# A transformer layer on one core: residual sums kept in the output by accumulating DMAs, and a down projection in 26 sums

## The chip, the core and the metric

The kernel runs on one core of a Trainium2 chip, as one program. The metric is the device time of one execution in microseconds (us). The instructions of each engine (TensorE "PE", VectorE "DVE", ScalarE "ACT", GpSimd "POOL", and SyncE "SP", which here only issues DMAs) run in the order in which they stand in that engine's program. They wait for each other through semaphores.

## What is computed

One layer of a hybrid encoder on 640 tokens (512 of a prompt, 128 of a sample), model width 2048, all in f32. Cut to what matters here:

```
a = rms_norm(x, g_mix);  proj = a @ w_in              # q, k, v, forget, ssm input
merged = concat(rms_norm(attention), rms_norm(s5))    # 2048 wide
h = x + merged @ w_out                                # stage "o"
f = rms_norm(h, g_ffn)
h = h + (silu(f @ w_gate) * (f @ w_up)) @ w_down      # stages "g", "u" and "d"
gate = sigmoid(rms_norm(h, g_ple) @ w_ple_gate)       # stage "p"
return h + gate * (p_i @ w_ple_proj)
```

## The kernel before

**Tiling.** Everything is kept transposed: rows are features, columns are the 640 tokens. From the o stage on, each f32 product is three matmuls, since every operand is cut into a high and a low part: wh by k0, wh by k1, wl by k0 (L1205, L1206, L1207). A block of two by two is multiplied with seven products instead of eight (Strassen in Winograd's form). The outputs of a stage come 256 rows at a time. One such pair of 128 rows, `j`, is one **sum** (`strassen`): seven PSUM tiles are accumulated over a number of weight **units**, each with 42 matmuls of 128x128 by 128x320, and then put together into a pair tile by two copies on ACT (L1232, L1234), six additions on DVE (L1233, L1235 to L1239) and one on POOL (L1240). The names say stage and sum: `o4` is the fifth sum of the o stage, `ro4` its result. All pair tiles (`r...`, `x...`, `hx...`, `hy...`, `pj...`) share two buffers.

**Stages.** o: 8 sums of 4 units. Then 22 times a g sum and a u sum, 4 units each. d: the down projection, 8 output pairs over 11 units each. An output pair's 11 units are cut into several sums (cells), because only 8 of the operand tiles `kt` fit; in the kernel before that is 28 sums in seven steps, each of them four pairs over the same units. p: 8 sums of 4 units.

**Weights.** `Ring` loads each unit (512 KB, SP queue, `wst`, two buffers), forms the Winograd combinations on DVE (`ws`, L109 to L112, four of 128x256), and cuts it: ACT writes `wh` (L86, one of 128x768 and one of 128x1024) and DVE writes `wl` (L87, the same two). `wh` and `wl` have two buffers, so a unit is cut while the two before it are in use. Units are numbered through the whole program: o is 84 to 115, d begins at 292, p is 380 to 411.

**What follows a sum.** In o the input rows `x` are read and added (L1280), the pair is stored to `h_dr`, scaled (ACT, L1267, twice 128x640), combined into the seven Winograd operands (`winograd_rows`, L118 to L121) and stored to `fc_dr`. Its squares go into the RMS sum (ACT L1249, DVE L1253 and L1254). The g stage later fetches these operands (`kf`) and cuts each into its two parts (`whole`: ACT L1050 and DVE L1051, a piece of 128x1280 and one of 128x960). In d all sums but a pair's last are added into `h_dr` by an accumulating DMA on the POOL queue (L1346). After a pair's last sum the rows are read back on the SP queue (`hx`), added (L1350), stored to `h_dr` (the profile gives `h2_dr` that name too), scaled, combined, and stored to `hc_dr` or cut directly (`kh`). In p each result is normalised, gated, multiplied by `pj`, and added on POOL to `hy`, the rows read back from DRAM (L1373). Then it is stored.

**Order.** A scheduler sets the order of each engine's instructions from dependencies and its own planned times; the text of the program gives priorities and no fixed order. A change of the text so moves instructions everywhere.

Of the kernel before, what the change touches and what calls it, by code (L numbers as in the profile page):

```python
# [9 lines left out]
F32 = mybir.dt.float32  # L10
# [4 lines left out]
OP = mybir.AluOpType  # L15
# [113 lines left out]
def down_cells():  # L129

    low, high = range(4), range(4, 8)
    steps = [(low, 0, 2), (high, 0, 4), (low, 2, 6), (high, 4, 8), (low, 6, 8), (high, 8, 11), (low, 8, 11)]
    return [(j, range(a, b), a == 0, b == FT // 4) for js, a, b in steps for j in js]

# [28 lines left out]
def hybrid_step(ctx: ExitStack, tc: tile.TileContext, io):  # L165
# [21 lines left out]
    cells = down_cells()  # L187
    units += [(1, io["w_down"][j, u]) for j, us, _, _ in cells for u in us]
    units += [(1, io["w_pg"][j, u]) for j in range(8) for u in (2, 3, 0, 1)]
    ring = Ring(nc, stp, units)  # L190
# [5 lines left out]
    m_dr = dp.tile([D, NTOK], F32, name="m_dr")  # L196
    h_dr = dp.tile([D, NTOK], F32, name="h_dr")
    h2_dr = dp.tile([D, NTOK], F32, name="h2_dr")
    tc_dr = dp.tile([FT // 2, P, 7, NH2], F32, name="tc_dr")
# [706 lines left out]
    def attention(h):  # L906
# [133 lines left out]
    def scale_group(s, name):  # L1040
# [135 lines left out]

    later = {}

    def fetch(name, slot, dram, i, late=False):
        k = kp_tile("k" + name, slot)  # L1180
        x = k[:, 1].bitcast(F32)
        nc.sync.dma_start(x, dram[i])
        if late:
            later.setdefault(i // 2 - 2, []).append(lambda: whole(k, x))
            return k
        return whole(k, x)

    def cut_late(u):
        for f in later.pop(u, ()):
            with tc.issue_after(ring.done[0]), tc.issue_after(ring.done[1]):  # L1190
                f()

    def products(name, kps, after=None, order=None):
# [74 lines left out]

    fk = []
    for j in range(8):  # L1270
        after = None
        if j == 7:
            def after(u):
                for i in (2 * u, 2 * u + 1):
                    if i < 7:
                        fk.append(fetch(f"f{i}", i, fc_dr, i, late=i == 6))
        r = strassen(f"o{j}", mk, after)
        x = pair(f"x{j}")
        nc.sync.dma_start(x, io["xT"][2 * j : 2 * j + 2].rearrange("a p n -> p a n"))
        nc.vector.tensor_tensor(r, r, x, op=OP.add)  # L1280
        c = seven(f"c{j}")
        scaled(c, r, gffn, j)
        if j < 7:
            keep(nc.vector, c, fc_dr, j)
        else:
            winograd_rows(nc.vector, c[:, :4], c[:, 4:])
            kf7 = kp_tile("kf7", 7)
            fk.append(kf7)
            later.setdefault(1, []).append(lambda: whole(kf7, c))
        nc.sync.dma_start(rows(h_dr, j), r)  # L1290
        squares(ssqh, r, x, j == 0)

# [9 lines left out]
    for f in range(FT // 2):  # L1302
        z = strassen(f"g{f}", fk, cut_late if f == 0 else None)
        if f == 0:
            scale_rows(ssqh, D)
        by_rows(z, ssqh)
        nc.scalar.activation(z, z, AF.Silu)
        after = None
        if f == FT // 2 - 1:
            def after(u):  # L1310
                if u < 2:
                    next_t()
        c = seven(f"t{f}")
# [8 lines left out]
    for j, us, _, _ in cells:  # L1322
        for u in us:
            uses[u] = uses.get(u, 0) + 1
    hk, hslot = {}, {4: 6, 5: 7, 6: 0, 7: 1, 0: 2, 1: 3, 2: 4, 3: 5}
    ready = []

    def next_h():
        i = ready.pop(0)
        hk[i] = fetch(f"h{i}", hslot[i], hc_dr, i)  # L1330

    for n, (j, us, first, last) in enumerate(cells):
        def after(i, us=us, n=n):
            uses[us[i]] -= 1
            if not uses[us[i]] and n < len(cells) - 4:
                next_t()
            if n < 2 and i:
                next_t()
            if n == len(cells) - 1:
                for _ in range(min(2, 3 - i)):  # L1340
                    if ready:
                        next_h()
# [8 lines left out]
        c = seven(f"hc{j}")  # L1351
        scaled(c, r, gple, j)
        if j in (3, 4, 5):
            winograd_rows(nc.vector, c[:, :4], c[:, 4:])
            hk[j] = whole(kp_tile(f"kh{j}", hslot[j]), c)
        else:
            keep(nc.vector, c, hc_dr, j)
            ready.append(j)
        nc.sync.dma_start(rows(h2_dr, j), r)
        squares(ssqp, r, x, j == 4)  # L1360
    hk = [hk[i] for i in (4, 5, 6, 7, 0, 1, 2, 3)]
    for j in range(7):
        z = strassen(f"p{j}", hk)
        if j == 0:
# [14 lines left out]
    nc.sync.dma_start(x, rows(pj_dr, 7))  # L1379
    nc.sync.dma_start(y, rows(h2_dr, 7))  # L1380
    ps = products("p7", hk, order=(1, 2, 6, 5, 3, 7, 4))
# [145 lines left out]
```

## Time and profile before

| | us |
|---|---|
| median of 3 runs | 2956.65 |
| lowest, highest | 2954.58, 2957.56 |
| the profiled execution | 2953.62 |
| its span from first to last instruction | 2951.8 |
| 0 to 801.5: input projection, attention, s5 | 801.5 |
| o, with its start | 801.5 to 1036 |
| g and u | 1036 to 2137 |
| d | 2137 to 2714 |
| p | 2714 to 2951.8 |

A time of the profile is counted from the span's start. TensorE is busy for 96% of the span, and its matmuls follow each other without a gap when nothing is missing; what can be lost or won are the places where it waits. PE's busy time counts a matmul as longer when the granted clock is lower, so a stretch is best read by its number of matmuls.

### The profile page before, as it was taken

What the parts mean: (1) busy time and instruction counts of PE and PEld (TensorE: products, weight loads), DVE (VectorE), ACT (ScalarE), POOL (GpSimd) and SP (SyncE); (2) the same over time, 40 slices, a digit from 0 to 9 for tenths busy, and PEclk for the clock granted to TensorE, in tenths of its full rate; (3) what the DMA queues carried; (4) which work ended last, traced back from release to release, by engine and by line L of the source; (5) the groups of instructions that cost most, each with busy time, mean ns of one, the idle gap of its engine ahead of it and who ended that gap; (6) DMA issues with size and microseconds to landing.
All of it is one profiled execution on the core that took longest, in us unless ns stands there. A gap on an engine that the chain in (4) does not pass through costs nothing. (4 is left out here: it accounts for less than half of the span.)

```text
span 2951.8 us, 47685 instructions
## 1 busy us (share of the span) xinstructions
PE 2827.2 (96%) x19051; PEld 2717.0 (92%) x19051; DVE 2265.6 (77%) x3912; ACT 1240.9 (42%) x1627; POOL 420.7 (14%) x463
## 2 busy tenths in 40 slices
PE   8899999998799989999999999999999999999998
PEld 6789998887789889999999999999989999998898
DVE  8939354455698888787878787878886877899888
ACT  4333365555643453333333333333433444355433
POOL 6612310001000001010101010101020100100111
PEclk9999999999989999999999999999999999999999
DMA  5565744547534633233323333333554445647444
GB/s 168 153 180 159 224 168 173 176 145 260 191 133 172 223 139 123 100 116 101 118 100 118 101 117 102 117 102 117 190 159 139 144 158 175 164 153 271 139 156 143
DMA packets 137487, 449.19 MB, mean 152 GB/s; under 512 B 14096, under 2 KB 34672, under 8 KB 124464
## 3 DMA queue, kind: packets, MB, share of 16 engines
q1 hardware_dynamic: 120032, 396.47, 39.2%
q0 software_dynamic: 15936, 45.47, 6.2%
q10 hardware_dynamic: 1296, 4.20, 0.4%
q8 instruction: 149, 2.44, 0.3%
q14 instruction: 74, 0.61, 0.1%
HBM read 342.25 MB, written 101.18 MB: 150 GB/s over the span
## 5 line engine op out<-in xcount | busy, mean ns | idle before, releaser
L86 ACT ACTIVATE wh<-wst 128x768 fp32r<-128x768 f32 x328 | 276.9, 845 | 659.3 <-issue 319.9
L87 DVE TENSOR_TENSOR wl<-ws,wh 128x1024 fp32r<-128x1024 f32 x328 | 421.0, 1284 | 101.4 <-ACT wh L86 101.0
L86 ACT ACTIVATE wh<-ws 128x1024 fp32r<-128x1024 f32 x328 | 344.6, 1051 | 358.9 <-DVE ws L112 358.9
L87 DVE TENSOR_TENSOR wl<-wst,wh 128x768 fp32r<-128x768 f32 x328 | 337.5, 1029 | 169.3 <-ACT wh L86 169.3
L1205 PE MATMUL d<-kt,wh 128*128 128x320 f32 x1232 | 383.6, 315 | 11.8 <-ACT wh L86 5.1
L1205 PE MATMUL g<-kf,wh 128*128 128x320 f32 x1232 | 381.6, 310 | 5.5 <-ACT wh L86 5.4
L1206 PE MATMUL g<-kf,wh 128*128 128x320 f32 x1232 | 381.1, 310 | 0.0
L1205 PE MATMUL u<-kf,wh 128*128 128x320 f32 x1232 | 380.3, 309 | 0.5 <-DVE rg L1236 0.4
L1206 PE MATMUL d<-kt,wh 128*128 128x320 f32 x1232 | 380.7, 312 | 0.0
L1206 PE MATMUL u<-kf,wh 128*128 128x320 f32 x1232 | 380.1, 309 | 0.0
L1207 PE MATMUL g<-kf,wl 128*128 128x320 f32 x1232 | 375.6, 310 | 4.4 <-DVE wl L87 4.4
L1207 PE MATMUL u<-kf,wl 128*128 128x320 f32 x1232 | 376.1, 309 | 0.6 <-DVE wl L87 0.6
L1207 PE MATMUL d<-kt,wl 128*128 128x320 f32 x1232 | 344.5, 315 | 7.4 <-DVE wl L87 7.3
L1205 PEld LDWEIGHTS d<-kt,wh 128*128 128x128 f32 x1232 | 235.1, 191 | 17.7 <-ACT wh L86 9.7
L1205 PEld LDWEIGHTS g<-kf,wh 128*128 128x128 f32 x1232 | 232.1, 188 | 6.8 <-ACT wh L86 6.8
L1207 PEld LDWEIGHTS g<-kf,wl 128*128 128x128 f32 x1232 | 230.2, 188 | 5.5 <-DVE wl L87 5.2
L1206 PEld LDWEIGHTS d<-kt,wh 128*128 128x128 f32 x1232 | 235.1, 191 | 0.0
L1207 PEld LDWEIGHTS d<-kt,wl 128*128 128x128 f32 x1232 | 224.8, 191 | 11.2 <-DVE wl L87 10.6
L1206 PEld LDWEIGHTS g<-kf,wh 128*128 128x128 f32 x1232 | 232.2, 189 | 0.0
L1205 PEld LDWEIGHTS u<-kf,wh 128*128 128x128 f32 x1232 | 231.2, 188 | 1.0 <-DVE rg L1236 0.7
L1206 PEld LDWEIGHTS u<-kf,wh 128*128 128x128 f32 x1232 | 231.2, 188 | 0.0
L1207 PEld LDWEIGHTS u<-kf,wl 128*128 128x128 f32 x1232 | 230.0, 188 | 0.9 <-DVE wl L87 0.9
(499 smaller groups left out, 5981.2 us busy)
## 6 DMA issues: line engine op xcount, KB each, us to landing
wst<-in_w_gate SPq DMA_DIRECT2D x88, 512.0 KB
wst<-in_w_up SPq DMA_DIRECT2D x88, 512.0 KB
wst<-in_w_down SPq DMA_DIRECT2D x88, 512.0 KB
tc_dr<-t SPq DMA_DIRECT2D x22, 1120.0 KB
kt<-tc_dr SPq DMA_DIRECT2D x22, 1120.0 KB
wst<-in_w_qk SPq DMA_DIRECT2D x32, 512.0 KB
kc<-in_cache_k SPq DMA_DIRECT2D x16, 1024.0 KB
vc<-in_cache_v SPq DMA_DIRECT2D x16, 1024.0 KB
```

Source lines behind the costliest of these rows:

```text
L86: a = nc.scalar.activation(wh[:, part], x, AF.Copy)
L87: b = nc.vector.tensor_tensor(wl[:, part], x, wh[:, part].bitcast(F32), op=OP.subtract)
L1205: nc.tensor.matmul(ps[i], wh[:, a, w], k[:, 0, b], start=f, stop=False)
L1206: nc.tensor.matmul(ps[i], wh[:, a, w], k[:, 1, b], start=False, stop=False)
L1207: nc.tensor.matmul(ps[i], wl[:, a, w], k[:, 0, b], start=False, stop=l)
```

## The change

1. Seven copies, x rows to the output `o_yT`, DRAM to DRAM, 640 KB each, are written into the attention loop on the POOL queue.
2. In o (sums 0 to 6) the addition of `x` and the store to `h_dr` go. The result is added into `o_yT` by an accumulating DMA of the POOL queue, and the sum is read back into a pair tile by a second DMA of that queue (`add_h`). Scaling, combining and squares work on that tile one sum later (`done_o`, after unit 1). The last sum is added on DVE.
3. The cutting of fetched operands is put off: `fetch` only notes it, and `cut_next` does one or two of them after later units.
4. d has 26 sums, in three groups of pairs, (4, 5), (0, 1, 6) and (7, 2, 3). A pair's last sum is also accumulated and read back one sum later; only the very last (pair 5) is added on DVE. Pairs 6 and 7 are cut directly, the others go through `hc_dr`; `kh4` is fetched on the POOL queue.
5. In p the reading of `hy`, the POOL addition and the store become one accumulating DMA.

```diff
-    low, high = range(4), range(4, 8)
-    steps = [(low, 0, 2), (high, 0, 4), (low, 2, 6), (high, 4, 8), (low, 6, 8), (high, 8, 11), (low, 8, 11)]
+    one, two, three = (4, 5), (0, 1, 6), (7, 2, 3)
+    steps = [(one, 0, 2), (two, 0, 3), (three, 0, 4), (one, 2, 6), (two, 3, 7), (three, 4, 8), (one, 6, 8),
+             (two, 7, 11), (three, 8, 11), (one, 8, 11)]
...
-    units += [(1, io["w_pg"][j, u]) for j in range(8) for u in (2, 3, 0, 1)]
+    units += [(1, io["w_pg"][j, u]) for j in range(8) for u in (3, 0, 1, 2)]
...
     for h in range(H):
+        if h:
+            nc.gpsimd.dma_start(io["o_yT"][2 * (h - 1) * P : 2 * h * P, :].rearrange("(a p) n -> a p n", p=P), xrow(h - 1))
...
+    def wait_cut(k, x):
+        uncut[id(k)] = tick[0], lambda: whole(k, x)
+        return k
...
-        return whole(k, x)
+        eng.dma_start(x, dram[i])
+        return wait_cut(k, x)
+
+    def cut_next(n=1, age=2):
+        for key in list(uncut)[:n]:
+            if tick[0] - uncut[key][0] >= age:
+                uncut.pop(key)[1]()
...
+    def add_h(r, j):
+        nc.gpsimd.dma_start(hrow(j), r, accum_op=OP.add)
+        x = pair(f"h{j}")
+        nc.gpsimd.dma_start(x, hrow(j))
+        return x
...
+    def done_o(x, j):
+        c = seven(f"c{j}")
+        scaled(c, x, gffn, j)
+        keep(nc.vector, c, fc_dr, j)
+        squares(ssqh, x, j == 0)
+
     for j in range(8):
...
+            if u == 1 and due:
+                due.pop()()
...
         r = strassen(f"o{j}", mk, after)
-        x = pair(f"x{j}")
-        nc.sync.dma_start(x, io["xT"][2 * j : 2 * j + 2].rearrange("a p n -> p a n"))
-        nc.vector.tensor_tensor(r, r, x, op=OP.add)
-        c = seven(f"c{j}")
-        scaled(c, r, gffn, j)
         if j < 7:
-            keep(nc.vector, c, fc_dr, j)
...
-        nc.sync.dma_start(rows(h_dr, j), r)
-        squares(ssqh, r, x, j == 0)
+            x = add_h(r, j)
+            due.append(lambda x=x, j=j: done_o(x, j))
...
+    def done_h(x, j):
+        c = seven(f"hc{j}")
+        scaled(c, x, gple, j)
+        if j in (6, 7):
+            winograd_rows(nc.vector, c[:, :4], c[:, 4:])
+            hk[j] = wait_cut(kp_tile(f"kh{j}", hslot[j]), c)
+        else:
+            keep(nc.vector, c, hc_dr, j)
+        squares(ssqp, x, j == 0)
...
         if not last:
-            nc.gpsimd.dma_start(rows(h_dr, j), r, accum_op=OP.add)
-            continue
-        x = pair(f"hx{j}")
-        nc.sync.dma_start(x, rows(h_dr, j))
-        nc.vector.tensor_tensor(r, r, x, op=OP.add)
...
-        nc.sync.dma_start(rows(h2_dr, j), r)
-        squares(ssqp, r, x, j == 4)
+            nc.gpsimd.dma_start(hrow(j), r, accum_op=OP.add)
+        elif not end:
+            x = add_h(r, j)
+            due.append(lambda x=x, j=j: done_h(x, j))
...
         nc.vector.tensor_tensor(z, z, x, op=OP.mult)
-        x = pair(f"hy{j}")
-        nc.sync.dma_start(x, rows(h2_dr, j))
-        nc.gpsimd.tensor_tensor(z, z, x, op=OP.add)
-        nc.sync.dma_start(rows(io["o_yT"], j), z)
+        nc.gpsimd.dma_start(hrow(j), z, accum_op=OP.add)
```

**What it does to the order.** First POOL at the program's start: `cb`, `dpad` and `zero` are tables being prepared, `ssq` and `xsq` the RMS sum of the input. Before:

```order
L317 MEMSET zero 128x1024
L408 MEMSET cb 128x2048
L269 TENSOR_TENSOR ssq<-ssq,xsq_169 128x640
L319 DMA dpad<-in_dskip 16x1024
L318 DMA k_dr<-zero 128x1024
L269 TENSOR_TENSOR ssq<-ssq,xsq_397 128x640
```

and now:

```order
L317 MEMSET zero 128x1024
L408 MEMSET cb 128x2048
L1021 DMA o_yT<-in_xT 16x10240 x2
L269 TENSOR_TENSOR ssq<-ssq,xsq_168 128x640
L1021 DMA o_yT<-in_xT 16x10240 x5
L319 DMA dpad<-in_dskip 16x1024
L318 DMA k_dr<-zero 128x1024
L269 TENSOR_TENSOR ssq<-ssq,xsq_396 128x640
```

The copies of the attention loop stand at the start, ahead of the DMAs for `dpad` and `k_dr` and of all but one of the `ssq` additions.

Second, ACT behind the sum o4, whose successor o5 has the units 104 to 107 (a `wh` from `wst` is the 128x768 piece, one from `ws` the 128x1024 piece). Before:

```order
L86 ACTIVATE wh104_9377<-ws104_9379 128x1024
L86 ACTIVATE wh105_9432<-wst105_9333 128x768
L1267 ACTIVATE c4_9459<-ro4_9445,c_g_ffn_134 128x640 x2
L1249 ACTIVATE x4_9456<-ro4_9445 128x1280
L86 ACTIVATE wh106_9520<-wst106_9388 128x768
L86 ACTIVATE wh105_9432<-ws105_9434 128x1024
L86 ACTIVATE wh106_9520<-ws106_9522 128x1024
L86 ACTIVATE wh107_9575<-wst107_9443 128x768
```

and now, from the same place on (L1265 is the squares' instruction, before L1249):

```order
L86 ACTIVATE wh105_9434<-wst105_9335 128x768
L86 ACTIVATE wh105_9434<-ws105_9436 128x1024
L86 ACTIVATE wh106_9510<-wst106_9390 128x768
L86 ACTIVATE wh106_9510<-ws106_9512 128x1024
L1290 ACTIVATE c4_9565<-h4_9459,c_g_ffn_133 128x640 x2
L86 ACTIVATE wh107_9576<-wst107_9445 128x768
L1265 ACTIVATE h4_9459<-h4_9459 128x1280
L86 ACTIVATE wh107_9576<-ws107_9578 128x1024
```

The scaling `c4` stood ahead of the first piece of unit 106; now it stands behind the whole of 106 and ahead of the first piece of 107, the last unit of o5. It reads `h4`, the tile read back, in place of `ro4`.

Third, ACT in the last part of d, behind the sum of pair 6 (`qd` and the rows `rd...<-d...` are the two copies of the sum that follows). Before:

```order
L1267 ACTIVATE hc6_25579<-rd22_25565,c_g_ple_136 128x640 x2
L1249 ACTIVATE hx6_25576<-rd22_25565 128x1280
L86 ACTIVATE wh366_25552<-ws366_25554 128x1024
L1232 ACTIVATE qd23_25764<-d23_1_25591 128x320
L86 ACTIVATE wh368_25695<-wst368_25563 128x768
L86 ACTIVATE wh367_25640<-ws367_25642 128x1024
L86 ACTIVATE wh368_25695<-ws368_25697 128x1024
L1234 ACTIVATE rd23_25763<-d23_3_25593 128x320
L86 ACTIVATE wh369_25750<-wst369_25651 128x768
L86 ACTIVATE wh369_25750<-ws369_25752 128x1024
L86 ACTIVATE wh370_25838<-wst370_25706 128x768
```

and now:

```order
L86 ACTIVATE wh367_25579<-wst367_25459 128x768
L86 ACTIVATE wh367_25579<-ws367_25581 128x1024
L1290 ACTIVATE hc6_25634<-h6_25528,c_g_ple_135 128x640 x2
L86 ACTIVATE wh368_25645<-wst368_25514 128x768
L1265 ACTIVATE h6_25528<-h6_25528 128x1280
L1248 ACTIVATE qd21_25714<-d21_1_25530 128x320
L1059 ACTIVATE kh6_25641<-hc6_25634 128x1280
L1250 ACTIVATE rd21_25713<-d21_3_25532 128x320
L1059 ACTIVATE kh6_25641<-hc6_25634 128x960
L86 ACTIVATE wh368_25645<-ws368_25647 128x1024
L86 ACTIVATE wh369_25700<-wst369_25590 128x768
L86 ACTIVATE wh369_25700<-ws369_25702 128x1024
```

The scaling `hc6` reads the tile read back, and the cutting of `kh6` (L1059), which was done from `hc_dr` much later, now stands right behind it, ahead of the second piece of unit 368.

## Rows read from the trace of the kernel before

**Rows 1.** the page, busy time, share of the span and instructions
```profile
PE 2827.2 (96%) x19051; PEld 2717.0 (92%) x19051; DVE 2265.6 (77%) x3912; ACT 1240.9 (42%) x1627; POOL 420.7 (14%) x463
```

**Rows 2.** stretches: PE, PEld, DVE, ACT, POOL busy (xcount), clock, DMA share, GB/s
```profile
898.70:1003.90 105.20, 99.83 (x673) 98.48 (x673) 88.21 (x149) 43.05 (x52) 3.50 (x4) 1.00 0.47 174
1003.90:1127.20 123.30, 107.94 (x694) 103.78 (x693) 107.24 (x163) 62.96 (x72) 9.61 (x8) 0.97 0.46 171
1127.20:2112.80 985.60, 985.60 (x6722) 985.60 (x6721) 814.42 (x1267) 347.90 (x420) 124.55 (x120) 1.00 0.33 110
2297.90:2578.30 280.40, 271.90 (x1808) 269.58 (x1807) 218.93 (x364) 109.84 (x133) 33.64 (x26) 0.98 0.54 155
2578.30:2713.76 135.46, 130.85 (x859) 125.69 (x858) 125.99 (x211) 66.03 (x80) 7.98 (x7) 1.00 0.54 184
2713.76:2786.20 72.44, 59.91 (x352) 56.61 (x351) 61.67 (x89) 37.98 (x42) 6.85 (x3) 0.91 0.53 197
2786.20:2915.10 128.90, 125.68 (x841) 123.17 (x841) 113.11 (x161) 46.41 (x55) 20.04 (x10) 1.00 0.46 160
```

**Rows 3.** the o stage after one sum's end: start, us, instruction [idle before]
```profile
905.24 0.47 DVE L1239 TENSOR_TENSOR ro<-ro,o 128x320 f32<-128x320 f32 x1
...
907.82 1.55 ACT L1267 ACTIVATE c<-ro,c_g_ffn 128x640 f32<-128x640 f32 x2 [5.28 <-DVE ro L1280]
...
910.44 0.83 ACT L86 ACTIVATE wh<-wst 128x768 fp32r<-128x768 f32 x1
...
911.32 0.42 PE L1205 MATMUL o<-km,wh 128*128 128x320 f32 x1 [1.34 <-ACT wh L86]
...
911.48 0.95 DVE L87 TENSOR_TENSOR wl<-wst,wh 128x768 fp32r<-128x768 f32 x1
```

**Rows 4.** POOL in the down stage, the same columns
```profile
2227.72 1.20 POOL L1346 DMA_DIRECT2D h_dr<-rd  x1 [2.80 <-issue]
...
2250.39 1.20 POOL L1346 DMA_DIRECT2D h_dr<-rd  x1 [0.84 <-POOL rd L1240]
```

**Rows 5.** the tile h_dr: durations of its instructions in ns, issue to landing
```profile
L1346 POOL DMA_DIRECT2D h_dr<-rd x20: 1195/1204/1305, 2168.9 to 2562.9; - x20
...
DMA to landing us min/median/max: 6.6/8.0/14.0
```

**Rows 6.** the DMA issues: KB each, median us to landing
```profile
db<-d_dr POOLq DMA_DIRECT2D x8, 512.0 KB, 5.2
```

**Rows 7.** groups by line in 2172.4:2637, DVE: busy, mean ns
```profile
L1051 DVE TENSOR_TENSOR kt<-kt 128x1280 fp32r<-128x1280 f32 x14 | 20.8, 1489 | 9.5 <-ACT kt L1050 9.5
L1051 DVE TENSOR_TENSOR kt<-kt 128x960 fp32r<-128x960 f32 x14 | 16.1, 1154 | 0.0
```

**Rows 8.** the start of the p stage, the columns of rows 3
```profile
2706.97 0.66 SPq L60 DMA_DIRECT2D wst<-in_w_pg  x1
...
2717.96 0.64 PE L1205 MATMUL p<-kh,wh 128*128 128x320 f32 x1 [3.89 <-ACT wh L86]
```

**Rows 9.** inside the p stage, the same columns
```profile
2799.07 1.22 DVE L87 TENSOR_TENSOR wl<-ws,wh 128x1024 fp32r<-128x1024 f32 x1
...
2799.18 0.38 SPq L1372 DMA_DIRECT2D hy<-h_dr  x1
...
2803.29 3.77 POOL L1373 TENSOR_TENSOR rp<-rp,hy 128x1280 f32<-128x1280 f32 x1 [10.59 <-DMA hy<-h_dr]
...
2804.47 3.40 DVE L87 TENSOR_TENSOR wl<-wst,wh 128x768 fp32r<-128x768 f32 x1 [0.24 <-ACT wh L86]
```

**Rows 10.** groups by line in 2786.2:2915.1: busy, mean ns
```profile
L87 DVE TENSOR_TENSOR wl<-ws,wh 128x1024 fp32r<-128x1024 f32 x20 | 36.3, 1817 | 11.4 <-ACT wh L86 11.3
```

**Rows 11.** table by stretch of the start, the columns of rows 2
```profile
10.00:20.00 10.00, 10.00 (x42) 8.03 (x41) 8.08 (x7) 5.42 (x9) 8.58 (x9) 1.00 1.01 374
20.00:50.00 30.00, 25.18 (x93) 18.96 (x92) 27.84 (x71) 18.63 (x27) 15.48 (x9) 0.89 0.47 156
60.00:90.00 30.00, 20.25 (x98) 16.07 (x97) 29.52 (x69) 4.32 (x7) 20.26 (x24) 0.88 0.37 102
```

More of the change, by code (lines that the diff above doesn't have):

```diff
@@ L1175, in whole, with fetch @@
         return k
-    later = {}
-    def fetch(name, slot, dram, i, late=False):
+    uncut, tick = {}, [0]
+    def wait_cut(k, x):
+        uncut[id(k)] = tick[0], lambda: whole(k, x)
+        return k
+    def fetch(name, slot, dram, i, eng=nc.sync):
         k = kp_tile("k" + name, slot)
         x = k[:, 1].bitcast(F32)
[L1182 to L1185, printed above, removed]
-        return whole(k, x)
[L1188 to L1191, printed above, removed]
+        eng.dma_start(x, dram[i])
[4 more added lines that the diff above has]
+                uncut.pop(key)[1]()
     def products(name, kps, after=None, order=None):
@@ L1310, in after @@
             def after(u):
-                if u < 2:
+                if u < 3:
                     next_t()
+                cut_next((0, 0, 2, 1)[u], 1)
         c = seven(f"t{f}")
@@ L1321, in hybrid_step @@
     uses = {}
-    for j, us, _, _ in cells:
+    for j, us, _ in cells:
         for u in us:
             uses[u] = uses.get(u, 0) + 1
[L1325 to L1333, printed above, removed]
+    hk, hslot = {}, {6: 6, 7: 7, 0: 0, 1: 1, 2: 2, 3: 3, 4: 4, 5: 5}
+    due = []
+    def done_h(x, j):
+        c = seven(f"hc{j}")
+        scaled(c, x, gple, j)
+        if j in (6, 7):
+            winograd_rows(nc.vector, c[:, :4], c[:, 4:])
+            hk[j] = wait_cut(kp_tile(f"kh{j}", hslot[j]), c)
+        else:
+            keep(nc.vector, c, hc_dr, j)
+        squares(ssqp, x, j == 0)
@@ L1334, in after, with next_h @@
+    def next_h(j, eng=nc.sync):
+        hk[j] = fetch(f"h{j}", hslot[j], hc_dr, j, eng)
+    for n, (j, us, last) in enumerate(cells):
+        end = n == len(cells) - 1
+        def after(i, us=us, n=n, end=end):
+            if i == 1 and due:
+                due.pop()()
             uses[us[i]] -= 1
-            if not uses[us[i]] and n < len(cells) - 4:
+            if not uses[us[i]] and us[-1] < FT // 4 - 1:
                 next_t()
-            if n < 2 and i:
+            if n == 0 and not i:
@@ L1338, in after @@
                 next_t()
[L1339 to L1342, printed above, removed]
+            if end:
+                if i == 1:
+                    due.append(pair("h5"))
+                    nc.sync.dma_start(due[0], hrow(5))
+                for k in ((0, 1), (2, 3), (4,))[i]:
+                    next_h(k, nc.gpsimd if k == 4 else nc.sync)
+            cut_next(1, 1 if n < 2 else 2)
         r = strassen(f"d{n}", [tk[i] for u in us for i in (2 * u, 2 * u + 1)], after)
@@ L1359, in hybrid_step @@
-        nc.sync.dma_start(rows(h2_dr, j), r)
-        squares(ssqp, r, x, j == 4)
-    hk = [hk[i] for i in (4, 5, 6, 7, 0, 1, 2, 3)]
+            nc.gpsimd.dma_start(hrow(j), r, accum_op=OP.add)
+        elif not end:
+            x = add_h(r, j)
+            due.append(lambda x=x, j=j: done_h(x, j))
+    x = due.pop()
+    nc.vector.tensor_tensor(x, x, r, op=OP.add)
+    c = seven("hc5")
+    scaled(c, x, gple, 5)
+    nc.gpsimd.dma_start(hrow(5), x)
+    winograd_rows(nc.vector, c[:, :4], c[:, 4:])
@@ L1362, in hybrid_step, with after_p0 @@
+    hk[5] = wait_cut(kp_tile("kh5", hslot[5]), c)
+    hk = [hk[i] for i in (6, 7, 0, 1, 2, 3, 4, 5)]
+    def after_p0(u, x=x):
+        if u == 1:
+            squares(ssqp, x, False)
+        cut_next(1, 0)
     for j in range(7):
-        z = strassen(f"p{j}", hk)
+        z = strassen(f"p{j}", hk, after_p0 if j == 0 else None)
         if j == 0:
@@ L1379, in hybrid_step @@
     nc.sync.dma_start(x, rows(pj_dr, 7))
-    nc.sync.dma_start(y, rows(h2_dr, 7))
+    nc.sync.dma_start(y, hrow(7))
     ps = products("p7", hk, order=(1, 2, 6, 5, 3, 7, 4))
```

67 lines of the change are left out of this document (37 added, 30 removed).

## The prediction

> **What bounds the kernel now.** I read the page first: TensorE is busy for 96% of the span [rows 1]. Then I cut the trace into stretches and counted matmuls in each, because a matmul has a fixed step when nothing is missing. Through the long g and u loop 6722 matmuls take 985.60 us, 0.1466 us each [rows 2], so a unit of 42 takes 6.16 us. What a stretch takes above its count times 0.1466 is its loss, clock drops included. By the other rows of the same table [rows 2]: four sums of o (898.7 to 1003.9) lose 105.2 - 673 x 0.1466 = 6.5 us, 1.6 for each sum; the end of o and the first g and u sums (1003.9 to 1127.2) lose 21.5; g and u nothing; the part of d with the four places where new `kt` are cut (2297.9 to 2578.3) loses 15.3; the last part of d (2578.3 to 2713.8) 9.5; the first sum of p with the end of its transition (2713.8 to 2786.2) 20.8; the other p sums (2786.2 to 2915.1) 5.6. The reader is to see there that DVE is nearly full (107 of 123, 126 of 135 us) in just these stretches, and at 83% in the g and u loop, which loses nothing. So the bound is TensorE, and what it loses it loses where DVE and ACT have, besides each unit's `wh` and `wl`, a burst of other work, or where they stand in line behind something that waits. The removable loss is about 80 us; the change goes at all of these places, and adds waits for DMAs in the same lines.
>
> **Start: seven copies.** They are new. By the order they stand on POOL at about 16 us, right where the DMA engines carry 374 GB/s at a share of 1.01 [rows 11]. 7 x 655,360 bytes = 4.6 MB take 12.3 us at that rate. In the 30 us after that the share is 0.47, so the engines have 16 us free: the copies fit, but the loads of `x` and weights beside them are late. DVE is busy for 27.8 of those 30 us and for 29.5 of the 30 from 60 on [rows 11], so what it loses it doesn't win back soon. Behind the copies on POOL's queue stand the `dpad` and `k_dr` DMAs and the `ssq` additions. Bounds: 0 (all in the free share) and +12 (all on the path). I take **+4.5**, nearer to the free share.
>
> **o, sums 0 to 6: the read-back.** Before, DVE adds `x` and the scaling follows. Now accumulate, read-back, scaling. Let T be the start of the next sum's first unit. In the trace PE waits for 1.34 us until 911.32 at that sum's second unit, so T = 911.32 - 1.34 - 6.16 = 903.8, and the last combination ends at 905.71 = T + 1.9 [rows 3]. The accumulating DMA is issued behind it, without delay or after POOL has sat idle for 2.8 us in place of 0.84 [rows 4]; I take 1.2 us. From issue to landing it takes 6.6 to 14.0, median 8.0, in d [rows 5]. The read-back waits for that; a POOL read of 512 KB takes 5.2 [rows 6], an SP read of 640 KB 4.1 until its reader starts [rows 9], and 5.2 x 640 / 512 = 6.5. I take 5.8. The tile is there at T + 1.9 + 1.2 + 8.0 + 5.8 = T + 16.9. When is it wanted? By the order, ACT's scaling stands ahead of the first `wh` of the next sum's last unit, which begins at T + 3 x 6.16 = T + 18.5. Behind the scaling (1.55) come that `wh` (0.83) and its `wl` (0.95), which PE wants some 0.3 after it starts [rows 3]: the tile is late from T + 18.5 + 0.3 - 1.55 - 0.83 - 0.95 = **T + 15.5** on. So a sum stalls for 1.4 us, and with some 0.4 for work that is ahead in the row when the tile lands (my choice) for 1.8, against 1.6 now: 7 x 0.2, **+1.5**. The DVE addition that goes (7 x 1.48) was work beside a PE that waits for ACT here, so it pays nothing by itself. Bounds: nothing late, -11; the read as slow as the accumulation, 8.0, +17.
>
> What the row shows on the size is 8.0 us for 640 KB with accumulation [rows 5]. The Trainium skill (DMA: Bandwidth & Descriptors, Anatomy of one DMA) fits a POOL DMA by 2.0 us plus bytes / 436e3, which gives 3.5 us as an estimate for each of the two transfers; the tile would come at about T + 10, nothing would stall, and this term would be -11. The trace does not agree for an accumulating one; no run here shows a 640 KB read on POOL.
>
> **End of o, first g.** The squares of the last sum go behind g0's second unit, and the operands are cut one by one. The loss of 21.5 us goes with DVE's excess of work, of which the change takes little (one set of squares, 1.6 us, is put later; the last sum's addition remains): **-2** (-4 to +1).
>
> **d, where `kt` are cut.** A tile costs DVE 1.489 + 1.154 = 2.6 us [rows 7]. Four of them in a row are 10.6 us, beside units of 6.16 us in which DVE has two `wl` (1.22 and 0.95) and four `ws` to make. Four such places make up the loss of 15.3, about 3.8 each. With `cut_next` and the new groups, by the order of DVE, two places stay as they are, at a third the four tiles are apart two by two, and the last two lie inside a sum. I take 1.5 places: **-5.5** (-9 to 0). What is late next there is nothing: steady d sums lose nothing. 26 sums instead of 28 also save two sets of combinations on DVE, beside other work: nothing.
>
> **d, last part.** Before, DVE is full (126.0 of 135.5) and 9.5 us are lost. Away go 7 x 1.48 us of DVE additions, which would pay nearly all of it. In comes the same wait as in o, 7 times, in the row of ACT ahead of a `wh`: 7 x about 1.2 us, less than in o since some sums have three units and others four, so the scaling stands at another place. `hc6` is the worst: the cutting of `kh6` now stands between the two pieces of unit 368, 2.2 us more of ACT. **-1** (-9 to +14).
>
> **p, first sum.** Now PE waits 3.89 us for unit 380, whose load was issued at 2706.97, behind two `kh` loads, and then runs at a lower granted clock, 0.91 over the stretch [rows 2, 8]. The load now stands ahead of the `kh` loads on SP. On the other side `kh0` to `kh5` are all cut here, and `kh4` is fetched on POOL behind the store of `hc4`: **-2** (-7 to +6).
>
> **p, the rest.** POOL's addition (3.77 us) goes. While it runs, DVE's `wl` takes 3.40 us instead of 0.95 [rows 3, 9], and the 20 wide ones take 1.817 on average, where an undisturbed one takes 1.22 [rows 9, 10]: 20 x 0.6 = 12 us of DVE. The loss of 5.6 us goes with it: **-5.2** (-5.6 to 0). The accumulating DMAs end long before the last sum's own stores.
>
> **Sum.** 4.5 + 1.5 - 2 - 5.5 - 1 - 2 - 5.2 = -9.7 us. The profiled execution took 2953.62 (span 2951.8); -9.7 gives 2943.9. The median of the runs, 2956.65, is 3.0 above it: **2947**, 0.3% faster. About 0.2%, 5.9 us, is what a measurement here can tell from no change.
>
> **Rivals.**
>
> *A. The read-back comes late (slower).* The tile is read back 14 times, in o and d, and each time ACT, and behind it the next `wh`, stands in line. Every us later than T + 16.9 costs 14 us; from T + 17.6 on (9.7 / 14 = 0.7 later) the whole gain is gone. For it: landings of up to 14.0 us [rows 5], and the POOL issue that is delayed by 2.8 [rows 4]. Against it: the median of 8.0 is narrow at the lower end, and the SP read of 4.1 [rows 9]. If the read takes 8.0 like the accumulation, 14 x 2.2 = 31 us: 2947 + 31 = **2978**.
>
> *B. The copies starve the start.* All 12 us on the path instead of 4.5: 2947 + 7.5 = **2954.5**, no change. For it: the full DMA engines and DVE [rows 11]. Against it: the free share behind. The Trainium skill (DMA: Bandwidth & Descriptors, Queues, rings and completion order) says that a DMA engine takes queues in turn, packet by packet; the trace of before has no second busy queue there to show it. By that rule the loads beside the copies go at half their pace, which is this rival.
>
> *C. The read-back is early.* Issue at once, 6.6, and 4.1: T + 1.9 + 6.6 + 4.1 = T + 12.6, ahead of T + 15.5. Neither o nor the tail then stalls: 14 x 1.8 = 25 us less, **2922**. The fit of the page above leads here too.
>
> *D. The cutting is not spread.* The change doesn't do at the `kt` places what it says, and the burst stays: 2947 + 5.5 = **2952.5**.
>
> **How the numbers follow.** Forecast 0.40, A 0.24, B 0.14, C 0.17, D 0.05. The forecast's own range is 2936 to 2958 (a few of the bounds above, together), most of it below 2950.7. Faster: 0.28 of the forecast, all of C, a third of B and half of D, 0.52. Slower (above 2962.6): nearly all of A and 0.04 of the rest, 0.27. No change: 0.21. The range reaches from C's value to a read-back 1.6 us late (2947 + 23): 2922 to 2970.
>
> **What would show it.** In the changed kernel: the time from a sum's end to ACT's scaling in o, with PE's wait at the last unit of the next sum; landing times of the accumulating DMAs (8.0) and of the read-back (5.8); the length of 20 to 50 us and the time at which o begins (801.5 now); the loss around each group of new `kt`; no `wl` above 1.3 us in p. A read-back at T + 19 or an o stage that begins 10 us late would make the prediction wrong; so would tail stalls of 3 us at each pair.

## The result and the profile after

The changed kernel takes 3000.9 us (median of 4 runs, 2994.9 to 3007.0), the kernel before in the same session 2955.6: a ratio of 1.0157, 95% interval 1.0144 to 1.0169. By that ratio it is 46 us slower; the median is 54 above the forecast and 31 above the top of the range. The profiled execution is the slowest of the four (3006.96, span 3005.2, 53.4 longer than that of before).

The table by stretch of the changed kernel, with the columns of [rows 2]; the stretches are those of [rows 2], with the start of o as the first row:

```profile
814.30:918.60 104.30, 83.97 (x506) 78.56 (x505) 83.75 (x140) 46.06 (x59) 5.78 (x6) 0.92 0.46 141
918.60:1031.10 112.50, 102.18 (x674) 100.08 (x673) 79.78 (x144) 41.94 (x53) 11.30 (x12) 0.98 0.57 162
1031.10:1158.70 127.60, 110.69 (x663) 105.90 (x662) 102.72 (x153) 61.32 (x68) 15.38 (x11) 0.89 0.48 169
...
2337.40:2593.90 256.50, 250.44 (x1665) 248.24 (x1665) 200.47 (x329) 102.38 (x122) 27.25 (x22) 0.98 0.54 156
2593.90:2767.50 173.60, 153.47 (x968) 148.87 (x967) 123.94 (x219) 67.65 (x82) 22.93 (x20) 0.94 0.52 149
2767.50:2845.20 77.70, 58.27 (x343) 54.91 (x342) 60.80 (x90) 40.86 (x45) 7.81 (x6) 0.85 0.57 194
2845.20:2969.30 124.10, 124.10 (x841) 123.10 (x841) 100.89 (x162) 46.63 (x55) 10.33 (x10) 1.00 0.49 136
```

That first stretch in the kernel before:

```profile
801.50:898.70 97.20, 81.77 (x491) 77.41 (x490) 85.38 (x139) 44.37 (x57) 1.76 (x2) 0.89 0.45 160
```

Length minus count times 0.1466, as in the prediction, gives the losses in us (g and u lose 0.3 at most, before and after):

| stretch | before | after |
|---|---|---|
| time at which o begins | 801.5 | 814.3 |
| o, first three sums | 25.2 | 30.1 |
| o, four sums | 6.5 | 13.7 |
| end of o, first g and u sums | 21.5 | 30.4 |
| d with the new `kt` | 15.3 | 12.4 |
| d, last part | 9.5 | 31.7 |
| first p sum | 20.8 | 27.4 |
| p, the rest | 5.6 | 0.8 |

DVE is less busy than before (123.9 of 173.6 us in the last part of d, where it was 126.0 of 135.5), while more is lost. So the amount of its work is not what costs.

**One sum of o.** Timeline of the changed kernel behind the sum o3 (start, us, instruction, and in brackets the idle time before it):

```profile
950.85 0.47 DVE L1255 TENSOR_TENSOR ro<-ro,o 128x320 f32<-128x320 f32 x1
...
951.88 1.20 POOL L1274 DMA_DIRECT2D o_yT<-ro  x1 [2.43 <-issue]
...
960.31 0.75 POOL L1276 DMA_DIRECT2D h<-o_yT  x1 [7.24 <-issue]
...
965.12 1.55 ACT L1290 ACTIVATE c<-h,c_g_ffn 128x640 f32<-128x640 f32 x2 [7.22 <-DMA h<-o_yT]
...
965.98 0.49 DVE L118 TENSOR_TENSOR c<-c 128x320 f32<-128x320 f32 x1 [6.03 <-ACT c L1290]
...
967.46 0.42 PE L1217 MATMUL o<-km,wh 128*128 128x320 f32 x1 [3.10 <-ACT wh L86]
...
979.56 0.47 DVE L1255 TENSOR_TENSOR ro<-ro,o 128x320 f32<-128x320 f32 x1
...
995.75 0.42 PE L1217 MATMUL o<-km,wh 128*128 128x320 f32 x1 [1.10 <-ACT wh L86]
```

The matmuls of o up to PE's wait at 967.46 (window, length, PE busy and count, clock, DMA share, GB/s):

```profile
814.30:967.45 153.15, 127.76 (x798) 0.94 0.49 145
```

A sum has 168 matmuls, and 798 is 4 x 168 + 126: PE waits 3.10 us just ahead of the last unit of the next sum, which so began at T = 967.46 - 3.10 - 18.48 = 945.9. The last combination (L1255) ends at 951.32, T + 5.4; the prediction has T + 1.9 for it, from [rows 3]. The accumulating DMA is issued at T + 6.0, the read-back at T + 14.4, and the tile is there at T + 19.2. ACT has then stood for 7.2 us, and DVE, whose next instruction needs what ACT makes, for 6.0.

The five sums at whose successor's last unit PE waits, read in the same way:

| sum | T | combination ends | tile is there | PE waits for `wh` |
|---|---|---|---|---|
| o1 | 888.5 | T + 5.8 | T + 19.8 | 3.7 |
| o2 | 918.8 | T + 4.4 | T + 17.5 | 1.4 |
| o3 | 945.9 | T + 5.4 | T + 19.2 | 3.1 |
| o4 | 976.2 | T + 3.9 | T + 17.2 | 1.1 |
| o5 | 1003.0 | T + 5.4 | T + 18.7 | 2.6 |

In each of them the tile is late from T + 16.1 on: what it comes later than that, PE waits. The combination ends at T + 5.0 on average, and a long wait is followed by an early combination, a short one by a late one.

The DMAs themselves were quicker than I took them. Issue to landing, first of the accumulating line of o and d, then of the read-back line:

```profile
DMA to landing us min/median/max: 6.2/7.7/15.7
```

```profile
DMA to landing us min/median/max: 4.3/4.6/9.7
```

7.7 us, 0.6 between, and 4.6: 12.9 in place of 13.8. The Trainium skill (DMA: Bandwidth & Descriptors, Anatomy of one DMA) gives by its fit 3.5 us as an estimate for each; the plain read comes near to that, the accumulating one takes twice as long.

**First p sum.** The last read-back of d runs beside the loads of `kh` (the timeline, and below it a wait of the SP queue between 2750 and 2800 us: in all, times, longest):

```profile
2758.21 1.19 POOL L1274 DMA_DIRECT2D o_yT<-rd  x1 [2.30 <-DVE ws L112]
...
2779.31 0.84 ACT L86 ACTIVATE wh<-wst 128x768 fp32r<-128x768 f32 x1 [2.11 <-DMA wst<-in_w_pg]
...
2780.20 0.63 PE L1217 MATMUL p<-kh,wh 128*128 128x320 f32 x1 [8.42 <-ACT wh L86]
...
2783.60 1.55 ACT L1290 ACTIVATE hc<-h,c_g_ple 128x640 f32<-128x640 f32 x2 [3.45 <-DMA h<-o_yT]
...
2789.82 0.64 PE L1217 MATMUL p<-kh,wh 128*128 128x320 f32 x1 [6.05 <-ACT rd L1250]
```

```profile
SPq L1395 <- DMA o_yT<-rd: 14.0, 1, 14.0
```

Accumulation and read together take 25 us here (2758.2 to 2783.6), and PE waits 8.4 and 6.1 us. The first of these two waits does not come from ACT standing for the tile, since that begins later. The rows of pair 5 are read on the SP queue (L1395), and this read stands there for 14.0 us until the accumulating DMA has landed. The weight load behind it in the queue is issued at 2774.5, and the `wh` that PE waits for is made from it. So a third line, that of SP, stands for the accumulation.

**The start.** The stretch from 20 to 50 us, what ACT waited for up to 75 us (in all, times, longest), and PE's longest wait:

```profile
20.00:50.00 30.00, 22.46 (x86) 16.66 (x85) 21.31 (x80) 12.11 (x17) 11.74 (x13) 0.89 0.82 279
```

```profile
ACT a L262 <- DMA x<-in_xT: 36.0, 7, 14.5
```

```profile
68.17 2.50 PE L512 MATMUL acc<-wh,a 128*128 128x512 f32 x5 [16.02 <-DVE a L263]
```

The DMA engines are at a share of 0.82 where they were at 0.47 [rows 11]. ACT waits up to 14.5 us for a load of `x` (4.7 in the kernel before), DVE falls from 27.8 to 21.3 us of work, and at 68 us PE stands for 16.

### The profile page after: what moved, and what is told of

Same layout as the page of the kernel before. It is cut to its first block, busy times and chain, and to the rows that moved or that the text cites. A ratio compares the mean times of both kernels' runs of the same rounds, so it can differ in the third digit from the quotient of the medians.

```text
span 3005.2 us, 47630 instructions
## 1 busy us (share of the span) xinstructions
PE 2842.3 (95%) x19051; PEld 2729.6 (91%) x19051; DVE 2221.8 (74%) x3886; ACT 1241.6 (41%) x1624; POOL 434.0 (14%) x497
## 5 line engine op out<-in xcount | busy, mean ns | idle before, releaser
L87 DVE TENSOR_TENSOR wl<-ws,wh 128x1024 fp32r<-128x1024 f32 x328 | 405.8, 1237 | 109.2 <-ACT wh L86 107.9
L87 DVE TENSOR_TENSOR wl<-wst,wh 128x768 fp32r<-128x768 f32 x328 | 331.0, 1009 | 169.2 <-ACT wh L86 169.0
L1217 PE MATMUL d<-kt,wh 128*128 128x320 f32 x1232 | 386.4, 317 | 24.1 <-ACT wh L86 17.6
L1217 PEld LDWEIGHTS d<-kt,wh 128*128 128x128 f32 x1232 | 237.5, 193 | 30.1 <-ACT wh L86 21.9
```

What stands on the lines that cost most here:

```text
L87: b = nc.vector.tensor_tensor(wl[:, part], x, wh[:, part].bitcast(F32), op=OP.subtract)
L1217: nc.tensor.matmul(ps[i], wh[:, a, w], k[:, 0, b], start=f, stop=False)
```

## The experiments

Ratios are to runs of the kernel before on the same chip, taken in the same session; us are what the ratio differs from 1 by, times 2955. The changed kernel stands at +46. With the intervals, a difference between two of these runs is uncertain by some 5 to 8 us.

| run | ratio, 95% interval | us |
|---|---|---|
| copies late | 1.0135 (1.0116 to 1.0154) | +40 |
| o as before | 1.0083 (1.0065 to 1.0101) | +25 |
| work on the read-back one unit later | 1.0113 (1.0087 to 1.0139) | +33 |
| ends of pairs in d as before | 1.0065 (1.0048 to 1.0081) | +19 |
| no copies, no read-backs | 0.9992 (0.9980 to 1.0004) | -2 |
| before, with p's accumulation alone | 0.9972 (0.9961 to 0.9984) | -8 |
| combinations of the read-back on POOL | 1.0153 (1.0129 to 1.0178) | +45 |
| before, with p's accumulation and cutting put off | 0.9977 (0.9967 to 0.9986) | -7 |
| before, with seven copies | 1.0019 (1.0009 to 1.0029) | +6 |
| before, with three copies | 1.0008 (0.9998 to 1.0018) | +2 |
| nobody scales from the read-back | 1.0040 (1.0025 to 1.0054) | +12 |

Several totals missed what was expected of them: the copies late gained 6 us (11 to 14 expected), o as before 21 (25 to 32), the work one unit later 13 (20 to 32), the combinations on POOL 1 (6 to 11), and seven copies cost 6 (10 to 13).

**Copies late.**

```diff
-        if h:
-            nc.gpsimd.dma_start(io["o_yT"][...], xrow(h - 1))
...
+        sent = nc.gpsimd.dma_start(io["o_kT"][h * P : (h + 1) * P, :], kT)
+        if h < 7:
+            with tc.issue_after(sent.ins):
+                nc.gpsimd.dma_start(io["o_yT"][...], xrow(h))
```

> The changed kernel, with the seven copies of x rows issued behind the store of each head's keys in the attention part (from about 240 us on) instead of at 16 us. Theory (the copies fill the DMA engines while the first inputs are loaded, which is where the 12.8 us up to the o stage come from): the o stage begins at 801 to 803 us, the total falls by 11 to 14 us against the changed kernel, to about 2988. Rival (the start is slower because the scheduler has set another order there, and the copies fit in free DMA time): o begins at 812 or later, the total stays within 3 us of the changed kernel.

The total is 6 us below the changed kernel (the two intervals overlap); in its profile o begins at 801.2. Its stretches 20 to 50 us and four sums of o:

```profile
20.00:50.00 30.00, 24.96 (x94) 19.01 (x93) 28.09 (x71) 18.63 (x27) 14.67 (x9) 0.89 0.47 157
908.40:1024.60 116.20, 105.58 (x673) 103.25 (x672) 80.59 (x145) 42.88 (x52) 11.29 (x12) 0.94 0.56 157
```

The start is that of before again (DVE 28.1, DMA share 0.47), and o is as bad as ever: 116.2 - 673 x 0.1466 = 17.5 us. So the start was the copies; by the runs they are worth half of what the one profile showed.

**The kernel before, with the copies and nothing else**, seven and three of them:

```diff
     for h in range(H):
+        if 0 < h <= 7:
+            nc.gpsimd.dma_start(io["o_yT"][...], io["xT"][2 * (h - 1) : 2 * h])
```

> The kernel before with the seven copies of x rows as the changed kernel has them at the start, and nothing else (p overwrites the rows later). Theory (the copies take the DMA engines from 17 to 37 us, the loads of x and weights come late, DVE idles there and never makes it good): o begins 10 to 13 us later than in the kernel before (801.5), the total is 10 to 13 us above it, and from o on nothing changes. Rival (the start of the changed kernel is slow through other edits): o begins within 3 us of 801.5.

> The same with three of the seven copies. Theory (engine time: 2.0 MB of 4.6 MB): 4 to 6 us above the kernel before. Rival (what costs is the other order that the scheduler sets for POOL's ssq additions and the s5 tables with seven copies, which it doesn't set with three): within 2 us of the kernel before.

Seven cost 6 us by the runs; in the profiled one o begins at 810.8. From 20 to 50 us:

```profile
20.00:50.00 30.00, 25.40 (x89) 19.27 (x88) 22.67 (x77) 10.87 (x15) 10.99 (x11) 0.83 0.77 270
```

The same picture without any other edit: DMA share 0.77, DVE 22.7. Three copies give +2, with an interval that includes no change: in proportion to their bytes (6 x 3/7 = 2.6), but not proof against the rival. In their profile o begins at 809.0. One profile says little of this stretch: o begins at 805.5 to 816.4 in the six profiles with seven copies at the start, and at 800.0 to 805.4 in the six with none there.

**o as before.**

```diff
-            x = add_h(r, j)
-            due.append(lambda x=x, j=j: done_o(x, j))
+        x = pair(f"x{j}")
+        nc.sync.dma_start(x, xrow(j).rearrange("a p n -> p a n"))
+        nc.vector.tensor_tensor(r, r, x, op=OP.add)
+        scaled(c, r, gffn, j)
...
+        nc.sync.dma_start(hrow(j), r)
```

> The changed kernel with the o stage of before: x read on SP, added on DVE, the pair stored on SP (into the output), scaled at once; no copies and no read-back in o. Theory (ACT and DVE stand in line behind the read-back, 13.6 us in o and some 5 behind it): o takes 234 to 238 us instead of 248, and with the start's 12.8 the total falls by 25 to 32 us, to about 2972. Rival (the o stage is slower through the traffic of the DMAs or the new cutting order, not through the wait): o stays above 243 us, and only the start's 13 us go, about 2988.

```profile
903.00:1008.30 105.30, 99.93 (x675) 98.60 (x674) 88.31 (x150) 43.06 (x52) 3.50 (x4) 1.00 0.47 174
```

The four sums of o lose 6.4 us, as before. Against the run with the copies late, which has the same quiet start, the o stage and what stands behind it are worth 40 - 25 = 15 us.

**Work on the read-back one unit later.** In o and d it now has to stand, on ACT and on DVE, behind the cutting of the next sum's last unit:

```diff
-            if u == 1 and due:
-                due.pop()()
+            if u == 2 and due:
+                with tc.issue_after(ring.done[0]), tc.issue_after(ring.done[1]):
+                    due.pop()()
```

> The changed kernel with the work on a read-back tile put behind the cutting of the next sum's last unit (one unit later on ACT and DVE, in o and in d); DMAs and amounts of work as they are. Theory (the tile lands at T + 19 to 22 and is wanted at T + 15.5; one unit later gives 6.2 us): the waits of ACT and DVE for it go, o takes 235 to 240 us, the last part of d loses 20 instead of 40 us, the total falls by 20 to 32 us, to about 2975. Rival (DVE has no room there, so that the loss only moves by a unit): the total stays within 6 us of the changed kernel.

Four sums of o, and the last part of d:

```profile
904.20:1011.30 107.10, 101.72 (x673) 98.73 (x674) 80.65 (x147) 43.20 (x54) 13.10 (x12) 1.00 0.57 171
2570.60:2745.40 174.80, 153.89 (x967) 149.00 (x967) 123.69 (x218) 67.63 (x82) 22.49 (x21) 0.94 0.53 151
```

In o the loss falls to 107.1 - 673 x 0.1466 = 8.4: the place in the line decides. In d it stays (33.0), against my expectation of 20. There most sums have three units, 18.5 us, and behind the last unit's cutting stands the first unit of the next sum, which wants its `wh` at that time:

```profile
2698.43 1.55 ACT L1290 ACTIVATE hc<-h,c_g_ple 128x640 f32<-128x640 f32 x2 [4.31 <-DMA h<-o_yT]
...
2700.76 0.41 PE L1217 MATMUL d<-kt,wh 128*128 128x320 f32 x1 [2.73 <-ACT wh L86]
```

ACT still waits 4.3 us for the tile, and PE for ACT. This is read from one place; what follows tests d by other means.

**Ends of pairs in d as before.**

```diff
-            x = add_h(r, j)
-            due.append(lambda x=x, j=j: done_h(x, j))
+            x = pair(f"hx{j}")
+            nc.sync.dma_start(x, hrow(j))
+            nc.vector.tensor_tensor(r, r, x, op=OP.add)
+            scaled(c, r, gple, j)
...
+            nc.sync.dma_start(hrow(j), r)
```

> The changed kernel with the end of each output pair in d as before: rows read on SP, added on DVE, stored on SP, scaled at once; the 26 sums in their new groups and everything else as changed. Theory (the 22.7 us that the last part of d loses are the seven read-backs): 15 to 25 us less, about 2980, with 7 x 1.48 us more DVE work. Rival (they come from the new groups, whose last sums of three units follow each other more closely and leave DVE less time per pair): less than 8 us, above 2993.

Last part of d, and the first p sum. As in the kernel before, the stretch of d ends where PE's first wait in p begins:

```profile
2591.80:2745.90 154.10, 146.96 (x960) 142.01 (x958) 135.85 (x226) 70.10 (x85) 7.06 (x7) 0.99 0.48 169
2745.90:2815.90 70.00, 59.20 (x350) 56.85 (x350) 60.72 (x93) 38.74 (x42) 5.56 (x5) 0.88 0.57 204
```

13.4 and 18.7 us lost in place of 31.7 and 27.4, with more DVE work (135.9 us) in less time. The seven read-backs of d are worth 46 - 19 = 27 us.

**No copies, no read-backs** (the edits of o and of d above, together).

> The changed kernel without any copies and read-backs: o and the ends of the output pairs as before, but the 26 sums in new groups, the cutting put off, and the accumulating DMAs of p as changed. Theory (what made it slower are the copies and the 14 read-backs, and the rest of the change gains): losses of about 38 us in o, 15 in d up to its last part, 21 and 15 in the last part and the first p sum, 14 in p: 3 to 10 us below the kernel before, about 2945. Rival (the order that the scheduler sets for the changed text costs something by itself, also without them): 2955 to 2965.

End of o with the first g and u sums, the last part of d, the first p sum, and PE's first wait in p:

```profile
1006.90:1132.00 125.10, 109.24 (x689) 104.90 (x688) 107.22 (x161) 61.77 (x70) 9.01 (x8) 0.96 0.46 168
...
2566.00:2718.50 152.50, 145.46 (x958) 140.29 (x958) 135.43 (x225) 70.14 (x85) 7.05 (x7) 1.00 0.50 170
2718.50:2788.70 70.20, 58.87 (x352) 55.73 (x351) 61.36 (x93) 38.77 (x42) 4.30 (x5) 0.93 0.58 205
```

```profile
2723.00 0.41 PE L1215 MATMUL p<-kh,wh 128*128 128x320 f32 x1 [4.12 <-ACT wh L86]
```

Losses of 24.1, 12.1 and 18.6 us. With 6 for the copies, 15 for o and 27 for d, the parts make 48, and the step from +46 to -2 is 48. The total is the same as before, although p gains (below). The last part of d loses 12.1 in place of 9.5, and the end of o 24.1 in place of 21.5. In this profile d begins 5.6 us later than in the one of before (2143.1, 2137.5); part of that can be the execution, since in the run with p's accumulation alone, which is the kernel before up to the end of d, it begins at 2135.4.

**Nobody scales from the read-back.** All DMAs are issued and all work is done as in the changed kernel, but the scaling takes the sum itself, so that the operands of g and p lack what was to be added (`x`, and the earlier part of h). Only the squares still read the tile, behind the last unit's cutting. The edit of d, which in o is the same:

```diff
-            due.append(lambda x=x, j=j: done_h(x, j))
+            due.append(lambda r=r, j=j: done_h(r, j))
+            due2.append(lambda x=x, j=j: squares(ssqp, x, j == 0))
```

> The changed kernel in which the scaling of the 14 pairs takes the sum itself in place of the tile read back (so the earlier residual is left out of the g and p operands; the amount of work on each engine stays), and only the squares still read that tile, behind the cutting of the next sum's last unit. All copies, accumulations and read-backs are issued as in the changed kernel. Theory (the wait in the line of ACT and DVE is what costs, in o and in the last part of d): four sums of o lose 6 to 8 us instead of 13.7, the last part of d 15 to 19 instead of 31.7 (16.4 without any read-back), the first p sum 14 to 20 instead of 27.4, the total falls by 25 to 42 us, to 2960 to 2975. Rival (the DMAs themselves, by traffic or by POOL's issues beside DVE, or the sums of three units cost it): the last part of d stays above 25.

Four sums of o, the last part of d, the first p sum; then ACT and PE in that p sum:

```profile
904.70:1010.70 106.00, 99.81 (x675) 98.62 (x674) 78.44 (x145) 43.08 (x52) 11.41 (x12) 1.00 0.55 173
2580.00:2735.70 155.70, 145.10 (x951) 141.99 (x950) 120.72 (x217) 68.58 (x82) 19.88 (x20) 0.98 0.56 164
2735.70:2811.30 75.60, 55.90 (x343) 53.37 (x342) 58.93 (x89) 39.70 (x43) 6.15 (x6) 0.89 0.57 198
```

```profile
2750.84 1.27 ACT L1265 ACTIVATE h<-h 128x1280 f32<-128x1280 f32 x1 [6.35 <-DMA h<-o_yT]
...
2752.89 0.63 PE L1217 MATMUL p<-kh,wh 128*128 128x320 f32 x1 [12.92 <-ACT wh L86]
```

7.0 us in o, as without any read-back (6.4), and 16.3 in the last part of d, where the changed kernel loses 31.7 and the run without read-backs 12.1. So in o the DMAs cost nothing by themselves, and in d the wait is 15.4 of the 19.6 us; where the other 4 come from is not shown. The first p sum still loses 25.3: the squares of the last pair wait 6.35 us for their tile in ACT's line, ahead of a `wh`, and PE stands for 12.9. The SP queue stands there too, for 12.4 us, and no run tells the two apart.

**Combinations of the read-back on POOL.**

```diff
-        keep(nc.vector, c, fc_dr, j)
+        keep(nc.gpsimd, c, fc_dr, j)
         squares(ssqh, x, j == 0)
```

> The changed kernel with one edit: in o the combinations of the tile read back (four of 128x320) run on POOL instead of DVE, so that DVE meets the read-back only with the squares, behind the ws of the next sum's last unit. Theory (the tile is late because DVE, held up by the previous read-back, ends the next sum's combinations at T + 4 to 8 instead of T + 1.9; the transfers themselves take 13 us): the combinations end at T + 2 to 3, the tile is there at T + 16 to 17, o loses 40 to 45 us instead of 51, total 6 to 11 us below the changed kernel. Rival (the transfers alone make it late; ACT's wait is enough): o still loses 49 us or more.

The same places as in the timeline above, behind the sum o5 (T = 1009.6):

```profile
1011.24 0.49 DVE L1255 TENSOR_TENSOR ro<-ro,o 128x320 f32<-128x320 f32 x1
...
1025.35 1.55 ACT L1290 ACTIVATE c<-h,c_g_ffn 128x640 f32<-128x640 f32 x2 [7.84 <-issue]
...
1028.24 1.37 DVE L1269 TENSOR_TENSOR ssqa<-ssqa,h 128x640 f32<-128x640 f32 x1 [7.89 <-ACT h L1265]
...
1029.53 1.61 DVE L87 TENSOR_TENSOR wl<-wst,wh 128x768 fp32r<-128x768 f32 x1
```

PE's waits from 880 to 1040 us, of the changed kernel and of this one (in all, times, longest):

```profile
PE o L1217 <- ACT wh L86: 11.8, 5, 3.7
PE o L1219 <- DVE wl L87: 3.2, 5, 1.0
```

```profile
PE o L1219 <- DVE wl L87: 8.9, 6, 1.7
PE o L1217 <- ACT wh L86: 8.9, 5, 2.5
```

The combination ends at T + 2.1 and the tile is there at T + 15.7 in this sum, 3.3 and 3.0 us earlier than behind the same sum of the changed kernel. In the other sums from o2 on the combination ends at T + 2.1 to 4.0. So DVE's line does set when the chain starts. But DVE has here not only no wait at the scaling, but also four combinations less to make, and the run doesn't tell the two apart. And nothing is won (+45): PE waits less for `wh` and more for `wl`. The scheduler now puts the squares ahead of the `wh`, DVE still waits 7.9 us in line for them, and beside POOL's combinations `wl` takes 1.61 us, not 0.95.

**The kernel before with p's accumulation alone**, and the same with the cutting of `kt` put off:

```diff
-        nc.sync.dma_start(rows(h2_dr, j), r)
+        nc.sync.dma_start(rows(io["o_yT"] if j < 7 else h2_dr, j), r)
...
-        nc.gpsimd.tensor_tensor(z, z, x, op=OP.add)
-        nc.sync.dma_start(rows(io["o_yT"], j), z)
+        nc.gpsimd.dma_start(rows(io["o_yT"], j), z, accum_op=OP.add)
```

> The kernel before with only the p stage changed: the result of each p sum added into the output by an accumulating DMA in place of read, POOL addition and store. Theory (DVE's wl run undisturbed when POOL adds nothing): p loses 14 to 16 us from its second sum on instead of 20.6, total 5 us below the kernel before. Rival (the loss in p has other causes): within 2 us of the kernel before.

> The kernel before with p as in the run with p alone, and besides the cutting of the kt tiles put off and spread as in the changed kernel; 28 sums, read-backs on SP as before. Theory: d loses 15 to 17 us up to its last part instead of 21.5, total about 10 us below the kernel before, near 2941. Rival (what d gains there comes from the 26 sums and their groups, not from the cutting): d loses 20 us or more, total as with p alone.

The first is the fastest kernel of this study: 0.9972, 8 us below the kernel before. Its p sums behind the first, and the wide `wl` in them (columns of [rows 10]):

```profile
2781.40:2905.40 124.00, 124.00 (x843) 123.20 (x842) 100.54 (x161) 46.64 (x55) 10.32 (x10) 1.00 0.48 135
```

```profile
L87 DVE TENSOR_TENSOR wl<-ws,wh 128x1024 fp32r<-128x1024 f32 x21 | 27.7, 1320 | 12.4 <-ACT wh L86 12.4
```

0.4 us lost in place of 5.6, and 1.32 us for a `wl` in place of 1.82. The second run gains nothing on top. Its stretch with the new `kt`:

```profile
2298.90:2578.70 279.80, 271.67 (x1808) 269.51 (x1807) 218.80 (x363) 109.70 (x132) 33.49 (x26) 0.98 0.54 155
```

279.8 us with 1808 matmuls, 14.7 lost, as before (15.3). The text of the program was changed, the order not. Counted in units of 42 matmuls from the start of d, the kernel before cuts four tiles each at 22.4 to 24.3, 38.2 to 40.2 and 54.2 to 56.2, and this one at the same places within 0.1. In the changed kernel four are cut at 23.2 to 25.1 and four at 55.4 to 57.3, and in between two at 31.7 and two at 43.5. So one of three places went, and 2.9 us with it. Whether the new groups or the cutting put off did that is not shown, since this run did not put the cutting off.

## Why the prediction was wrong, point by point

- **o, sums 0 to 6 (+1.5): the step that failed.** The mis-sized term is the first of the chain, "the last combination ends at 905.71 = T + 1.9", because T was counted wrongly. PE's wait at 911.32 was taken for the start of the sum's second unit. The count of o's matmuls up to there, in the kernel before:

```profile
801.50:911.31 109.81, 93.00 (x564) 0.91 0.44 156
```

564 is 3 x 168 + 60, so the wait comes 60 matmuls into the sum and not 42, and T = 911.32 - 1.34 - 60 x 0.1466 = 901.2. Two other rows agree: DVE starts to read the last product of the sum before at 902.27 (L1238), so that sum had ended by then; and the `wh` behind the scaling belongs to the third unit in the order shown for o4. The combination ends at T + 4.5 in the kernel before already. With that the prediction's own terms give the tile at T + 19.5, 4 us late and not 1.4. The runs showed T + 17.2 to 19.8: the combination at T + 5.0 on average, the rest of the chain 13 to 14 us in place of 15.0. Late is from T + 16.1 on (15.5 predicted). So the place of the wait was right, and quick DMAs made up for a part of the miscount, by luck.

DVE waits as well, which the prediction left out, and not for little (o stage; in all, times, longest):

```profile
DVE c L118 <- ACT c L1290: 41.5, 7, 7.9
```

By the table of five sums this puts the combination off by about half a us on average against the kernel before, and the waits do not grow from sum to sum. With scaling taken from the sum, four sums of o lose 7.0, with the wait 13.7; by the runs o and what follows cost 15 us.
- **d, last part (-1).** The price "7 x about 1.2 us, less than in o" failed too. 31.7 us are lost, 16.3 when nobody scales from the tile, 12.1 without read-backs: 15.4 for six waits, 2.6 each, where o has 1.7 (13.7 less 7.0, for four). Five of the seven sums that follow a pair's last one have three units, so that their last unit comes 6 us sooner; how much of the difference that makes is not shown. That the relief of DVE "would pay nearly all" of 9.5 failed as well: in the run in which nobody scales from the tile DVE is relieved of the additions, and more is lost than in the one that has them.
- **End of o (-2) and first p sum (-2).** The last read-back of each stage was priced like the others; it runs beside the loads of the next stage's operands, and in p SP's line stands for it too: 30.4 in place of 21.5, and 27.4 in place of 20.8. Without read-backs the first p sum loses 18.6, 2.2 less than before, as forecast, but not for the reason given: PE's first wait in p, which the order of loads was to shorten, is 4.1 us there and was 3.9.
- **Start (+4.5; 0 to 12).** 6 us by the runs. The profile alone (12.8) would have misled.
- **d with new `kt` (-5.5).** 2.9 gained. The kernel before has three places with four tiles and one with two, not four with four, and one of the three went, not 1.5.
- **p, the rest (-5.2).** Right in place and cause: 4.8 there, 8 by the runs for the edit alone.
- **Rivals.** A was the case, with its place; its price (14 x 2.2 = 31 us on top of the forecast) was too low. It starts from the same T, takes d's waits for o's, and has nothing for the last read-backs. B was half the case (6 of 12 us). C was not: none of the five tiles was early. Of D, the cutting stayed in a burst at two of three places.

## What to carry to other kernels

A wait that is moved into the line of an in-order engine has to be priced against the time at which something queued behind it is wanted, and this for every line in which it stands (here ACT, DVE and SP) and every length of sum. Both ends of that comparison must be counted from the same point. Fix the point by counting matmuls: a wait of PE does not say by itself which unit it belongs to, and 18 matmuls, 2.6 us in each sum, were hidden that way. And test the parts of a change by themselves: one of five edits, on its own, is faster than both kernels.

## What the runs showed of the hardware

An accumulating DMA of 640 KB took 7.7 us from issue to landing in o and d (6.2 to 15.7), a plain read of the same size on the same queue 4.6 (4.3 to 9.7). POOL's elementwise work slowed DVE's: 1.61 us for a `wl` of 128x768 beside the last of POOL's combinations of 128x320, and 3.40 beside its addition of 128x1280 [rows 9], against 0.95 [rows 3].
